# Input rows of a hybrid decoder step loaded in quarter-row transfers for pairs of token blocks

## The chip, the cores and the metric

The kernel runs on one core of a Trainium2 chip. The metric is the device time of one execution in microseconds (us); the profiler's record of one execution gives, beside it, the span from its first to its last instruction. Engines are named as in the profile: PE is TensorE (PEld its weight loads), DVE is VectorE, ACT is ScalarE, POOL is GpSimd, SP is SyncE, which here only issues transfers (DMAs).

## What is computed

One inference step of a hybrid decoder layer: a Mamba-2 branch and a gated-linear-attention branch, merged by gates, then cross-attention into 256 memory tokens, then a causal ConvFFN. The tokens are 256 of a prompt and 32 of a sample group (8 sequences of 4), 288 in all, with 2048 channels. The change lies in the first 110 us, where two things are computed side by side. One is the keys and values of the prompt's memory:

```python
def _mem_kv(mem, norm_mem, w_ck, w_cv):
    mn = _rmsnorm(mem, norm_mem)
    k = (mn @ w_ck).reshape(Bsz, N_MEM, CROSS_HEADS, CROSS_HEAD_DIM)
    v = (mn @ w_cv).reshape(Bsz, N_MEM, CROSS_HEADS, CROSS_HEAD_DIM)
```

The other is the first norm of the layer, `xn = _rmsnorm(x, p['norm_mix'])`, whose result, turned so that channels lie on partitions, is what all input projections multiply.

## The kernel before

**Weights.** All weights are float32 and stream from HBM once. `wload` (L108) brings a piece of 128 x 2 x 512 numbers (512 KB) into one of three `raw` buffers (`RB = 3`), on SP's queue. `wsplit` (L100) makes two parts of each half of a piece: ACT casts it to `whi` (L103), DVE subtracts to get `wlo` (L105). There are five buffers of each (`WB = 5`). PE then does six matmuls of 128 x 512 for each half in `mem_proj` (L321, L322, L325). A new piece may be issued when DVE has made the second `wlo` of the piece three places ahead, whose buffer it takes over. So PE, ACT, DVE and SP form a loop through three buffers.

**The stage of the change.** `mem_proj` runs first for head 0 of `w_ck` (it also loads the memory tokens into `mt`), then L467 weaves four more projections (`w_cv` head 0, `w_ck` head 1, `w_cv` head 1, `w_ck` head 2: 32 pieces in all) with a background generator, one step of it for about one half piece. The background is `x_norm` (L388) and then `x_prep` (L435).

**The input rows.** `xrow` (L362) is a tile of 128 x 9 x 512: nine blocks of 32 tokens. Token t of a block has the i-th quarter of its row (512 channels, 2 KB) on partition 32 i + t. `x_load(n)` (L382) loads one block, the sample's first (block 8), then the prompt's blocks 0 to 7, at steps 3, 6, 9, ... 27 of `x_norm`. At step 12 `square` begins: for each block ACT sums squares (L393) and DVE turns 32 x 32 squares of it into `xT` (L395), block 8 first, then 0 to 7 at steps 15 to 36. Once all are there, one matmul (L429) spreads the sums, and `x_prep` scales, splits and stores x (L439 to L443).

**What sets the order.** The steps are written out by hand in program order. SP issues in that order: each weight piece and each x transfer stands in one line, and an instruction that waits holds all those behind it. SP's transfers count their landings on eight semaphores in turn (DMAHW0 to DMAHW7), so a transfer also can't be issued before the one eight places ahead of it on the queue has landed. An x load depends on nothing but its place on the queue and on `mt`, whose memory `xrow` takes over.

Of the kernel before, what the change touches and what calls it, by code (L numbers as in the profile page):

```python
# [42 lines left out]
def hybrid_step(ctx: ExitStack, tc: tile.TileContext, I: dict, O: list):  # L43
    ctx.enter_context(tc.block(schedule_with_timeline_sim=True))
    nc = tc.nc
# [20 lines left out]
    def mm_tile():  # L66
        return ps.tile([P, 512], F32, tag="mm", bufs=3, name="mm")
# [27 lines left out]
    def vec(name):  # L95
        o, n = vofs[name]
        return vcol[:, o:o + n]
# [174 lines left out]
    with pool("p0") as p0:  # L272
# [89 lines left out]
        xrow = p0.tile([P, 9, 512], F32, tag="rows", name="xrow")  # L362
# [18 lines left out]

        def x_load(n):  # L382

            b = n - 1 if n else 8
            src = I["x_prompt"][0, 32 * b:32 * b + 32] if n else I["x_sample"].rearrange("b l d -> (b l) d")
            tc.keep_in_program_order(nc.sync.dma_start(out=xrow[:, b, :], in_=src.rearrange("t (i d) -> i t d", i=4)))

        def x_norm():  # L388
            ss = p0.tile([P, 9], F32, name="ss")

            def square(b):
                junk = p0.tile([P, 512], F32, name="junk")
                tc.keep_in_program_order(S.activation(junk, xrow[:, b, :], ACT.Square, accum_out=ss[:, b:b + 1]))  # L393
                tc.keep_in_program_order(
                    V.transpose(xT[:, :, 32 * b:32 * b + 32], xrow[:, b, :].rearrange("p (x j) -> p j x", j=KT)))  # L395

            for step in range(37):
                if step % 3 == 0 and 3 <= step <= 27:
                    x_load(step // 3 - 1)
                if step == 3:  # L400

                    V.tensor_reduce(mrs, mss, AX.X, ALU.add)
                    S.activation(mrs, mrs, ACT.Ln, scale=1.0 / D, bias=epsc[:, 0:1])
                    S.activation(mrs, mrs, ACT.Exp, scale=-0.5)
                if step == 6:
                    held.pop()()
                if step % 3 == 0 and step >= 12:
                    square(step // 3 - 5 if step > 12 else 8)
                yield
            yield  # L410
            a = mm_tile()
            TR(a[:, 0:r], vrow[0:r, :], ident[0:r, 0:r])
            TR(a[:, 128:224], crow, ident[0:96, 0:96])
            yield
            V.tensor_copy(vcol[:, 0:r], a[:, 0:r])
            V.tensor_scalar(scw, a[:, 128:224], 0.5, None, ALU.mult)
            ob, nb_ = vofs["ssd_conv_b"]
            V.tensor_scalar(vcol[:, ob:ob + nb_], vcol[:, ob:ob + nb_], 0.5, None, ALU.mult)
            V.tensor_scalar(rg, vec("gla_norm"), 0.5, None, ALU.mult)
            for e in range(2):  # L420
                V.tensor_copy(dcol[64 * e:64 * e + 64, :],
                              drow[64 * e:64 * e + 64, :].rearrange("p (t e) -> p e t", e=2)[:, e, :])
            yield

            dg = p0.tile([P, 9, NS], F32, name="dg")
            V.tensor_tensor(dg, fold4.unsqueeze(1).to_broadcast([P, 9, NS]), ss.unsqueeze(2).to_broadcast([P, 9, NS]), ALU.mult)
            yield
            a = mm_tile()
            MM(a[:, 0:T], ones, dg.rearrange("p c t -> p (c t)"), start=True, stop=True)  # L429
            S.activation(rtok, a[:, 0:T], ACT.Ln, scale=1.0 / D, bias=epsc[:, 0:1])  # L430
            S.activation(rtok, rtok, ACT.Exp, scale=-0.5)
# [22 lines left out]
        for c in range(4):  # L454
# [11 lines left out]
        V.tensor_copy(gmask, gm_f)  # L466
        weave(chain(*(mem_proj(*a) for a in ((I["w_cv"], 0, o_pmv), (I["w_ck"], 1, o_pmk), (I["w_cv"], 1, o_pmv),  # L467
                                             (I["w_ck"], 2, o_pmk)))), chain(x_norm(), x_prep()), 4 * KT - 2, 59)


# [772 lines left out]
    for n in range(8):  # L1243
        kind, i = units[n]
# [64 lines left out]
    for q in range(4):  # L1309
        m = pc.tile([P, 4, T], F32, tag="mar", bufs=2, name="mar")  # L1310
# [288 lines left out]
    for i in range(5):  # L1599
        src = I["ffn_conv_w"][i] if i < 3 else I["ffn_conv_b"] if i == 3 else I["norm_final"]  # L1600
# [223 lines left out]
```

## Time and profile before

| | before |
|---|---|
| time, median of 3 runs | 2531.62 us (2530.82 to 2531.65) |
| time of the profiled execution | 2531.55 us |
| its span | 2529.8 us |
| PE busy | 2499.2 us, 99% of the span |
| DVE, ACT, POOL busy | 1755.3, 1336.4, 393.3 us |
| moved by DMA | 521.95 MB, mean 206 GB/s |

The span is 1.75 us shorter than the execution's own time. Times in the trace count from the span's start. Rows of the windows view give, for a stretch, each engine's busy time and instructions, the granted TensorE clock (1.00 is full), the mean busy share of the 16 DMA engines, and what they moved. In the views of waits a row reads: who waited, for whom, total us, times, longest. In the timeline a bracket at the end of a row gives the idle time before it and what ended it. In the chain of waits, a DMA row lasts from the issue of a transfer to its landing.

### The profile page before, as it was taken

Reading aid. Unit: us, or ns where it says so; the run is one execution under the profiler, and the core shown is the slowest. Engines: PE = TensorE matmul, PEld = TensorE weight load, DVE = VectorE, ACT = ScalarE, POOL = GpSimd, SP = SyncE. Lnnn points to the kernel's source line nnn. Section 1 sums busy time; section 2 is a strip of 40 time slices with the busy share of each in tenths; the row PEclk is TensorE's granted clock in tenths of the full one; section 3 lists DMA queues with packets and bytes.
Section 4 is the critical chain, followed back from the end, with each engine's and each line's share of the span. In section 5 each row is a group of like instructions: output and inputs, shape, how many; then the busy total and the mean of one; then the engine's idle time right before and its main releaser. Section 6 shows DMA issues by size and latency. Waiting matters only on the chain.

```text
span 2529.8 us, 50295 instructions
## 1 busy us (share of the span) xinstructions
PE 2499.2 (99%) x18866; PEld 2405.9 (95%) x18866; DVE 1755.3 (69%) x3757; ACT 1336.4 (53%) x2714; POOL 393.3 (16%) x728
## 2 busy tenths in 40 slices
PE   8999999999999999999999999999999999999998
PEld 7789999999999999999999988999999999999998
DVE  5766677787867656666666677667777677675765
ACT  5655647655363645454454544555555455454545
POOL 3011043332300000000001112402111001020010
PEclk9999999999999999999999999999999999999999
DMA  7766687867868676767677698655555555555554
GB/s 228 255 197 194 179 250 205 232 190 231 236 188 271 184 244 182 247 204 264 205 227 244 197 329 316 210 164 174 169 173 169 170 171 173 167 171 172 169 170 129
DMA packets 442009, 521.95 MB, mean 206 GB/s; under 512 B 26768, under 2 KB 390128, under 8 KB 441732
## 3 DMA queue, kind: packets, MB, share of 16 engines
q1 hardware_dynamic: 407716, 422.34, 54.6%
q0 software_dynamic: 34016, 96.38, 11.9%
q8 instruction: 148, 2.42, 0.4%
q14 instruction: 97, 0.79, 0.1%
q10 hardware_dynamic: 32, 0.01, 0.0%
HBM read 473.13 MB, written 45.48 MB: 205 GB/s over the span
## 4 chain that ended last, share of the span: by engine, by line
PE 90%; DMA 5%; DVE 2%; ACT 1%; issue 1%; POOL 0%; SPq 0%; DVEq 0%; ACTq 0%
PE acc L148 26%; PE acc L147 26%; PE acc L151 26%; PE acc L321 2%; PE acc L325 2%; PE acc L322 2%; DMA raw<-in_w_cv_dram 1%; DMA raw<-in_w_ck_dram 1%; DVE wlo L105 1%; PE mm L1152 1%; PE la L1143 1%; PE la L1476 1%; DMA raw<-in_w_in_dram 1%; PE mm L1116 1%; DMA raw<-in_w_cq_dram 1%
## 5 line engine op out<-in xcount | busy, mean ns | idle before, releaser
L103 ACT CAST whi<-raw 128x512 fp32r<-128x512 f32 x1464 | 895.1, 618 | 1034.1 <-PE acc L148 759.0
L105 DVE TENSOR_TENSOR wlo<-raw,whi 128x512 fp32r<-128x512 f32 x1464 | 996.4, 688 | 614.2 <-ACT whi L103 599.9
L147 PE MATMUL acc<-xn,whi 128*128 128x288 f32 (+1 forms) x1936 | 550.6, 300 | 0.0
L148 PE MATMUL acc<-xn,whi 128*128 128x288 f32 (+1 forms) x1936 | 542.6, 296 | 0.0
L151 PE MATMUL acc<-xn,wlo 128*128 128x288 f32 (+1 forms) x1936 | 414.1, 295 | 0.0
L148 PE MATMUL acc<-hf,whi 128*128 128x288 f32 x1408 | 393.5, 296 | 0.0
L147 PE MATMUL acc<-hf,whi 128*128 128x288 f32 x1408 | 389.1, 292 | 0.0
L147 PEld LDWEIGHTS acc<-xn,whi 128*128 128x128 f32 (+1 forms) x1936 | 364.7, 188 | 9.9 <-issue 8.3
L148 PEld LDWEIGHTS acc<-xn,whi 128*128 128x128 f32 (+1 forms) x1936 | 365.1, 189 | 6.6 <-issue 4.6
L151 PEld LDWEIGHTS acc<-xn,wlo 128*128 128x128 f32 (+1 forms) x1936 | 311.1, 188 | 1.7 <-issue 1.3
L151 PE MATMUL acc<-hf,wlo 128*128 128x288 f32 x1408 | 295.0, 290 | 0.0
L148 PEld LDWEIGHTS acc<-hf,whi 128*128 128x128 f32 x1408 | 265.0, 188 | 0.1
L147 PEld LDWEIGHTS acc<-hf,whi 128*128 128x128 f32 x1408 | 264.3, 188 | 0.1
L151 PEld LDWEIGHTS acc<-hf,wlo 128*128 128x128 f32 x1408 | 226.6, 188 | 0.0
L148 PE MATMUL acc<-pr,whi 128*128 128x288 f32 x704 | 196.7, 296 | 0.0
L147 PE MATMUL acc<-pr,whi 128*128 128x288 f32 x704 | 195.0, 293 | 0.0
L151 PE MATMUL acc<-pr,wlo 128*128 128x288 f32 x704 | 147.7, 290 | 0.0
L147 PE MATMUL acc<-un,whi 128*128 128x288 f32 x512 | 145.5, 300 | 1.4 <-DVE mb L954 1.2
L148 PE MATMUL acc<-un,whi 128*128 128x288 f32 x512 | 143.1, 295 | 0.0
L1648 POOL COPY fsp<-fst 128x16 f32<-128x16 f32 x88 | 37.1, 425 | 656.1 <-DVE av L1660 402.1
L148 PEld LDWEIGHTS acc<-pr,whi 128*128 128x128 f32 x704 | 132.5, 188 | 0.0
L147 PEld LDWEIGHTS acc<-pr,whi 128*128 128x128 f32 x704 | 132.1, 188 | 0.0
(507 smaller groups left out, 4265.3 us busy)
## 6 DMA issues: line engine op xcount, KB each, us to landing
raw<-in_w_in_dram SPq DMA_DIRECT2D x240, 512.0 KB
raw<-in_w_up_dram SPq DMA_DIRECT2D x176, 512.0 KB
raw<-in_w_down_dram SPq DMA_DIRECT2D x88, 512.0 KB
raw<-in_w_cv_dram SPq DMA_DIRECT2D x32, 512.0 KB
raw<-in_w_ssd_out_dram SPq DMA_DIRECT2D x32, 512.0 KB
sin<-in_state_gla_dram POOLq DMA_DIRECT2D x32, 512.0 KB, 6.0
out_dram<-sin SPq DMA_DIRECT2D x32, 512.0 KB
raw<-in_w_gla_out_dram SPq DMA_DIRECT2D x32, 512.0 KB
```

The source lines that it names most:

```text
L103: S.copy(hi, raw)
L105: V.tensor_tensor(lo, raw, hi, ALU.subtract)
L147: MM(a, hi[:, k, cs], xh, start=(k0 + s0 + k == 0), stop=False)
L148: MM(a, hi[:, k, cs], xl, start=False, stop=False)
L151: MM(a, lo[:, k, cs], xh, start=False, stop=(k0 + s0 + k == nk - 1))
L321: MM(accs[m], mn_hi[:, kk, ms_], hi[:, 0, :], start=(kk == 0), stop=False)
L322: MM(accs[m], mn_lo[:, kk, ms_], hi[:, 0, :], start=False, stop=False)
L325: MM(accs[m], mn_hi[:, kk, ms_], lo[:, 0, :], start=False, stop=(kk == KT - 1))
L1116: MM(a, kt[:, i, k * P:(k + 1) * P], vt[i], start=True, stop=True)
L1143: MM(osa[NS * j:NS * j + NS, :], qdm[:, k, b, :], sins[b][:, k, :], start=False, stop=(q == 1 and k == 0))
L1152: MM(a, kb[:, k * P:(k + 1) * P], vst, start=True, stop=True)
L1648: G.tensor_copy(sp[:, :, 0:2], st.rearrange("p (b k) -> p b k", k=2))
```

## The change

`x_load` now loads two blocks of the prompt at once (the sample's block alone), and does so with four transfers, one for each quarter of the row: 32 partitions, on each 2 x 2 KB. Before, it was one transfer for a block, with the quarters as the outermost dimension (4), then 32 tokens, then 512 channels. Now the outermost dimension of each transfer is 32. The loads stand at steps 3 (sample), 6, 12, 18 and 24. Bytes and places in SBUF are the same; 9 transfers become 20.

```diff
         def x_load(n):
-            b = n - 1 if n else 8
-            src = I["x_prompt"][0, 32 * b:32 * b + 32] if n else I["x_sample"].rearrange("b l d -> (b l) d")
-            tc.keep_in_program_order(nc.sync.dma_start(out=xrow[:, b, :], in_=src.rearrange("t (i d) -> i t d", i=4)))
+            b, m = (2 * n - 2, 2) if n else (8, 1)
+            src = I["x_prompt"][0, 32 * b:32 * b + 64] if n else I["x_sample"].rearrange("b l d -> (b l) d")
+            for i in range(4):
+                tc.keep_in_program_order(nc.sync.dma_start(
+                    out=xrow[32 * i:32 * i + 32, b:b + m, :],
+                    in_=src[:, 512 * i:512 * i + 512].rearrange("(b t) d -> t b d", t=32)))
...
             for step in range(37):
-                if step % 3 == 0 and 3 <= step <= 27:
-                    x_load(step // 3 - 1)
+                if step == 3 or step % 6 == 0 and 6 <= step <= 24:
+                    x_load(step // 6)
```

On PE, DVE, ACT and POOL every instruction stands where it stood; only lines behind L386 move by three. On SP, this is the queue at the start of the woven stage, before (`raw` is a weight piece, `xrow` an x load; x3 means three such in a row):

```order
17 L114 DMA raw<-in_w_cv_dram 128x2x512 x3
18 L386 DMA xrow<-in_x_sample_dram 128x1x512
19 L114 DMA raw<-in_w_cv_dram 128x2x512
20 L386 DMA xrow<-in_x_prompt_dram 128x1x512
21 L114 DMA raw<-in_w_cv_dram 128x2x512 x2
22 L386 DMA xrow<-in_x_prompt_dram 128x1x512
23 L114 DMA raw<-in_w_cv_dram 128x2x512
24 L386 DMA xrow<-in_x_prompt_dram 128x1x512
25 L114 DMA raw<-in_w_cv_dram 128x2x512
26 L114 DMA raw<-in_w_ck_dram 128x2x512
27 L386 DMA xrow<-in_x_prompt_dram 128x1x512
28 L114 DMA raw<-in_w_ck_dram 128x2x512
```

And the same place on SP with the change:

```order
17 L114 DMA raw<-in_w_cv_dram 128x2x512 x3
18 L387 DMA xrow<-in_x_sample_dram 32x512 x4
19 L114 DMA raw<-in_w_cv_dram 128x2x512
20 L387 DMA xrow<-in_x_prompt_dram 32x2x512 x4
21 L114 DMA raw<-in_w_cv_dram 128x2x512 x3
22 L387 DMA xrow<-in_x_prompt_dram 32x2x512 x4
23 L114 DMA raw<-in_w_cv_dram 128x2x512
24 L114 DMA raw<-in_w_ck_dram 128x2x512 x2
25 L387 DMA xrow<-in_x_prompt_dram 32x2x512 x4
26 L114 DMA raw<-in_w_ck_dram 128x2x512 x4
27 L387 DMA xrow<-in_x_prompt_dram 32x2x512 x4
```

The weight pieces stand in the same order; a group of four x transfers comes after every third or fourth of them, where one came after every one or two.

With the semaphores that each waits for, the same queue from the sample's load on, before (DVE is the wait for the `raw` buffer, a DMAHW number the wait for a landing):

```order
20 L386 DMA xrow<-in_x_sample_dram 128x1x512 [waits DMAHW6_49,DMAHW0_49,PE_49]
21 L114 DMA raw<-in_w_cv_dram 128x2x512 [waits DMAHW2_49,DVE_49]
22 L386 DMA xrow<-in_x_prompt_dram 128x1x512
23 L114 DMA raw<-in_w_cv_dram 128x2x512 [waits DMAHW3_49,DVE_49]
24 L114 DMA raw<-in_w_cv_dram 128x2x512 [waits DMAHW4_49,DVE_49]
```

And with the change, where the piece just ahead of the sample's load counts on DMAHW4 and the sample's four on DMAHW5, 6, 7 and 0:

```order
20 L387 DMA xrow<-in_x_sample_dram 32x512 [waits DMAHW6_49,DMAHW0_49,PE_49]
21 L387 DMA xrow<-in_x_sample_dram 32x512 x3
22 L114 DMA raw<-in_w_cv_dram 128x2x512 [waits DMAHW2_49,DVE_49]
23 L387 DMA xrow<-in_x_prompt_dram 32x2x512
24 L387 DMA xrow<-in_x_prompt_dram 32x2x512 [waits DMAHW3_49]
25 L387 DMA xrow<-in_x_prompt_dram 32x2x512 [waits DMAHW4_49]
26 L387 DMA xrow<-in_x_prompt_dram 32x2x512 [waits DMAHW5_49]
27 L114 DMA raw<-in_w_cv_dram 128x2x512 [waits DMAHW6_49,DVE_49]
28 L114 DMA raw<-in_w_cv_dram 128x2x512 [waits DMAHW7_49,DVE_49]
```

The third and fourth transfer of the first pair now wait for the landing of that piece and of the sample's first transfer, and the next weight piece stands behind them.

## The prediction

> **What bounds the kernel now.** I read the page first, then the waits of PE, then the windows of the stage where those waits lie, then the chain of waits, then DMA shares in windows of a few us.
>
> ```profile
> PE 2499.2 (99%) x18866; PEld 2405.9 (95%) x18866; DVE 1755.3 (69%) x3757; ACT 1336.4 (53%) x2714; POOL 393.3 (16%) x728
> ...
> PE acc L321 <- ACT whi L103: 9.7, 7, 1.6
> ...
> core 0: us, PE busy (x) PEld busy (x) DVE busy (x) ACT busy (x) POOL busy (x), PEclk, DMA share, GB/s
> 41.00:90.00 49.00, 39.33 (x165) 29.91 (x164) 24.81 (x36) 22.23 (x46) 0.73 (x1) 1.00 0.66 211
> 90.00:140.00 50.00, 50.00 (x244) 42.28 (x243) 39.00 (x77) 32.71 (x67) 7.74 (x19) 1.00 0.79 248
> 140.00:240.00 100.00, 100.00 (x550) 87.53 (x549) 58.57 (x108) 56.57 (x107) 9.99 (x24) 1.00 0.69 208
> ```
>
> PE bounds the kernel. Of its 30.6 us without work (2529.8 less 2499.2), 9.7 are in seven waits for `whi`, all between 41 and 90 us, which is when the x loads run; from 90 to 240 us PE is never idle. So this stage is where an x load can cost or bring time. What does `whi` wait for? The waits of ACT from 41 to 90 us and one stall in the timeline answer it:
>
> ```profile
> ACT whi L103 <- DMA raw<-in_w_ck_dram: 12.9, 5, 3.9
> ACT whi L103 <- DMA raw<-in_w_cv_dram: 11.1, 4, 4.3
> ...
> 34.18 0.38 SPq L114 DMA_DIRECT2D raw<-in_w_cv_dram  x1
> 34.61 0.58 SPq L386 DMA_DIRECT2D xrow<-in_x_prompt_dram  x1
> 35.29 0.43 SPq L114 DMA_DIRECT2D raw<-in_w_cv_dram  x1
> ...
> 42.94 1.14 ACT L103 CAST whi<-raw 128x512 fp32r<-128x512 f32 x2 [4.31 <-DMA raw<-in_w_cv_dram]
> 43.61 0.51 PE L321 MATMUL acc<-whi,mn_hi 128*128 128x512 f32 x1 [1.59 <-ACT whi L103]
> ```
>
> For landings of weights. The piece issued at 34.18 us, behind the sample's x load, is cast only at 42.94, and PE starts 1.59 us late. How long pieces fly, and what the loop through the three buffers adds, is in the chain of waits (a DMA row lasts from issue to landing):
>
> ```profile
> 32.87 4.54 DMA raw<-in_w_cv_dram
> ...
> 39.46 9.14 DMA raw<-in_w_cv_dram
> ...
> 49.42 7.93 DMA raw<-in_w_cv_dram
> ...
> 64.50 7.65 DMA raw<-in_w_ck_dram
> ...
> 72.26 0.63 ACT whi L103
> ...
> 73.52 0.70 DVE wlo L105
> 74.23 11.44 DMA raw<-in_w_ck_dram
> ...
> 88.10 0.23 PE acc L321
> ...
> 89.46 0.23 PE acc L321
> ```
>
> PE needs 89.46 - 88.10 = 1.36 us for six matmuls, a half piece, so 2.73 us for a piece and 8.18 us for the three in the buffers. From a landing (64.50 + 7.65 = 72.15) to the next issue into that buffer (74.23) go 2.08 us. So PE is fed as long as a piece flies no longer than 8.18 - 2.08 = **6.1 us**. The four long flights have a mean of 9.04: the loop then gives a piece every (9.04 + 2.08)/3 = 3.71 us. Measured: 165 matmuls are 13.75 pieces in 49 us, 3.56 us each. The loop explains the stage within 4%.
>
> Why 8 to 11 us, when 4.54 occurs? DMA shares in stretches inside the stage, against one with x stores and weights but no x load:
>
> ```profile
> 44.50:45.00 0.50, 0.50 (x4) 0.41 (x3) 0.39 (x1) 0.00 (x0) 0.00 (x0) 1.00 0.26 94
> 58.00:60.00 2.00, 1.88 (x8) 1.58 (x9) 1.90 (x4) 1.90 (x6) 0.00 (x0) 1.00 0.26 102
> 68.00:70.50 2.50, 2.49 (x10) 1.70 (x10) 1.52 (x3) 2.50 (x6) 0.73 (x1) 1.00 0.26 102
> 79.00:81.00 2.00, 1.94 (x9) 1.20 (x7) 1.16 (x2) 0.00 (x1) 0.00 (x0) 1.00 0.26 101
> 100.00:120.00 20.00, 20.00 (x91) 16.48 (x90) 15.45 (x31) 13.57 (x28) 0.71 (x1) 1.00 0.97 336
> ```
>
> A share of 0.26 is 4.2 of 16 engines, at 102 GB/s: for 2 us at a time four engines work and twelve are empty. Four is the outermost dimension of the x transfer. So 256 KB take 2.6 us on four engines, and a weight piece, which has a part on all 16, lands only when its parts behind that x load are through, with the next x load queued behind it again. From 100 to 120 us, x stores of 288 KB (128 partitions) lie between the same weight pieces at 336 GB/s, and PE is busy for all 20 us.
>
> **The change, part by part.** *Removed: the queue on four engines.* With 32 outermost, I take each quarter transfer to spread over 16 engines. No row of before shows an x transfer of this shape, so its speed is bounded: below by the four-engine rows (102 GB/s), above by the full-width y stores at the end; the nearest row is that of the last y store, of 32 partitions, alone in the second window:
>
> ```profile
> 2522.83 2.39 SPq L1780 DMA_DIRECT2D out_dram<-y  x2
> ...
> 2525.00:2526.50 1.50, 0.00 (x0) 0.00 (x0) 0.00 (x0) 0.00 (x0) 0.00 (x0) 0.50 1.00 401
> 2527.50:2528.00 0.50, 0.00 (x0) 0.00 (x0) 0.00 (x0) 0.00 (x0) 0.00 (x0) 0.50 1.24 295
> ```
>
> I take 295 GB/s: a pair of blocks (512 KB) is 1.8 us of all engines, once in three or four pieces. A piece right behind it flies at most 4.54 + 1.8 = 6.3 us, the others 4.54; the mean, about 5, is under the bound of 6.1, and the five `whi`/`wlo` buffers (five half pieces, 6.8 us of PE) absorb one late piece. So PE should be fed throughout.
>
> The Trainium skill, page "DMA: Bandwidth & Descriptors", section "Why a DMA increments its semaphore by 16 and not by 1", says that a transfer runs on the largest number of engines up to 16 that divides the outermost sizes of both sides. By it the transfers go from 4 engines to 16; the row of 0.26 agrees for the 4, and no run here shows the 16 yet.
>
> What is that worth? At PE's pace, 165 matmuls take 165 x 1.364/6 = 37.4 us of the 49, so **11.6 us** are lost. This is more than the 9.7 us of waits, since in each of seven stalls PE also drains (0.39 less 0.23 us) and restarts slowly (0.51 less 0.39): 7 x 0.28 = 2.0, sum 11.7.
>
> *Added: issues on SP.*
>
> ```profile
> L386 SPq DMA_DIRECT2D xrow<-in_x_prompt_dram x8: 558/569/1012, 34.6 to 72.2; - x8
> L386 SPq DMA_DIRECT2D xrow<-in_x_sample_dram x1: 737/737/737, 33.3 to 33.3; - x1
> ...
> L114 SPq DMA_DIRECT2D raw<-in_w_cv_dram x32: 367/368/427, 25.5 to 194.5; - x32
> ...
> L507 SPq DMA_DIRECT2D acum_d<-acumT x1: 344/344/344, 148.8 to 148.8; - x1
> ...
> L601 SPq DMA_DIRECT2D out_dram<-cst x16: 737/792/848, 238.7 to 577.9; - x16
> ```
>
> A quarter transfer lies between 0.34 (L507, 32 partitions) and 0.79 us (L601, 3 or 24 partitions). I take 0.4, near L507 and the weight pieces: 20 x 0.4 = 8.0 against 0.74 + 8 x 0.57 = 5.3 us, 2.7 more on SP in 49 us, of which its weight issues take 14 x 0.37. SP has room. A weight piece behind a group comes 4 x 0.4 = 1.6 us later instead of 0.57, which lies inside the cushion of the buffers. At 0.79 the group holds it 3.2 us, still less.
>
> *Added: waits on SP.* The third and fourth transfer of the first pair wait for the piece of 32.87 (landed 32.87 + 4.54 = 37.41) and for the sample's first quarter. Behind them on SP stand the weight pieces. The next, issued at 35.29 before, then goes at 37.41 + 2 x 0.4 = 38.2 and lands at 42.8. PE wants it 2.73 us after 41.86 (where it now stalls: 43.61 less 1.59, less 0.16 of drain), so its cast must start by 44.6 - 0.67 = 43.9. 1.1 us are to spare; with 6.1 us of flight it would be 0.4 late. In later groups the transfer eight places ahead lies three weight pieces back, 3 x 2.73 = 8.2 us, and has landed. For this and single late pieces I leave **0.6 us** (bounds 0 and 5.8, half of the loss).
>
> *Moved: arrival of x.* Odd blocks come three steps earlier, none later. The first use is far behind:
>
> ```profile
> 53.66 0.63 ACT L393 ACTIVATE junk<-xrow 128x512 f32<-128x512 f32 x1
> ```
>
> The sample's load was issued 20 us ahead. Nothing is won or lost here.
>
> **Sum**, against the profiled execution (2531.55 us: span 2529.8 and 1.75 around it; the median, 2531.62, is 0.07 above): 2531.55 - 11.6 + 0.6 = **2520.6 us**. PE then goes on 11 us earlier, and between 90 and 240 us nothing makes it wait that isn't itself driven by this chain.
>
> **Rivals.** (1) *Only half is won*: weights still fly 7.5 us, because quarter transfers move slower than I take. The loop gives (7.5 + 2.08)/3 = 3.19 us a piece, 13.75 x (3.19 - 2.73) = 6.3 us remain, and the time is 2531.55 - 5.3 = **2526.2**. For it: the share of 1.24 at 295 GB/s, packets slower than those of full-width stores. Against it: x is a quarter of the stage's bytes (9 x 256 KB beside 14 x 512 KB). The Trainium skill, "SBUF — State Buffer", section "Door 1: The DMA port swizzle", says that 32 partitions reach 8 of the 16 ports, so such a transfer runs at half rate, about 218 GB/s. By that, my estimate is 2.4 us for a pair where the row of 295 GB/s gives 1.8; the row of the last y store agrees that it is slower, but by a quarter, not a half.
>
> (2) *The gain is given back*: PE, 11 us earlier, meets something with a time of its own, and ends near **2531.5**. Against it: no wait of PE from 90 to 240 us, and buffers set when later loads start.
>
> (3) *Slower*: the transfers do not do what the change says and still go over four engines. Then flights stay near 9 us, nothing is won, and the new wait bites: the third transfer stands on SP until 32.87 + 9.0 = 41.9, the next piece is issued at 42.7 and lands at 51.7, where PE wants it at 43.9: some 7.8 us, against about 1 us of stall that this piece has now, so **2538.4**. It decides once flights stay above 6.1 us on the mean. Against it: the share follows the outermost dimension, and 0.26 fits 4.
>
> **Chances.** Forecast 0.72 (2519 to 2523), (1) 0.13 (2523 to 2527), (2) 0.07 (2527 to 2532), (3) 0.08 (2532 to 2540). A measurement of this kernel tells some 0.2%, 5.1 us, from no change: faster means below 2526.5. The forecast and nearly all of (1) lie there: faster 0.84, same 0.09, slower 0.07. The range is 2518.8 (all of 11.6 and 1 us more, from matmul records that may be missing in 165) to 2526.5, which leaves out (2), (3) and the edge of (1).
>
> **What will show it.** Right: no stretch at a share of 0.26 and 102 GB/s in the stage; PE's waits for `whi` there fall from 9.7 us to under 2; ACT's waits for `raw` shrink; four x issues in a row of about 0.4 us; the spread matmul (L429 before) starts some 11 us earlier. Wrong: shares of 0.26 still there (rival 3), or shares over 1 while PE still waits (rival 1), or PE's waits gone here and as much idle time behind 90 us (rival 2).

## The result, and the profile after

The changed kernel takes 2519.92 us (median of 4 runs, 2516.15 to 2523.97), against 2531.22 (4 runs, 2529.74 to 2531.65) before: a ratio of 0.9957, with a 95% interval of 0.9939 to 0.9974. Two later sets of runs, each beside new runs of before, gave 0.9971 (0.9957 to 0.9985) and 0.9967 (0.9956 to 0.9979). So it is faster by 0.3 to 0.4%, 7 to 11 us. The forecast was 2520.6. The 65 runs of before in the later sets have medians of 2527.14 to 2529.04 us, and all lie between 2520.79 and 2536.57 but for one slow run of 2718.35 us; so the four runs of before in the first set lie high, and the first difference, 11.3 us, is the largest of the three (the others are 7.7 and 6.9).

The profiled execution of the changed kernel is the longest of its four, 2523.97 us, span 2522.2. Read again the waits of PE over the whole span (us, number of waits, the longest):

```profile
PE mm L890 <- ACT cst L599: 2.4, 1, 2.4
PE acc L321 <- ACT whi L103: 2.2, 3, 1.6
```

and the window of the stage, with the busy time of each engine, the granted clock, the DMA share and GB/s:

```profile
41.00:90.00 49.00, 46.64 (x200) 36.65 (x199) 31.36 (x46) 27.99 (x58) 1.45 (x2) 1.00 0.84 248
```

The waits for `whi` fell from 9.7 us in seven to 2.2 in three, and are no longer the longest of the kernel. In the same 49 us PE does 200 matmuls instead of 165; at 0.227 us each 3.5 us are still lost where 11.6 were. DMA moves 248 GB/s in the stage instead of 211, and no stretch at a share of 0.26 and 102 GB/s is left between 33 and 99 us. The spread matmul that ends the stage (`dg`, 128x288) comes 8.2 us earlier; the first row is of before, the second of after:

```profile
L429 PE MATMUL mm<-dg,ones x2: 403/405/407, 107.0 to 107.2; 128*128 128x288 f32 x2
```

```profile
L432 PE MATMUL mm<-dg,ones x2: 403/405/407, 98.8 to 99.1; 128*128 128x288 f32 x2
```

Where SP issues x, and what flights of weights the chain of waits still shows between 30 and 90 us of the changed kernel:

```profile
32.71 0.37 SPq L114 DMA_DIRECT2D raw<-in_w_cv_dram  x1
33.18 1.80 SPq L387 DMA_DIRECT2D xrow<-in_x_sample_dram  x4
35.08 0.38 SPq L114 DMA_DIRECT2D raw<-in_w_cv_dram  x1
35.51 2.16 SPq L387 DMA_DIRECT2D xrow<-in_x_prompt_dram  x4
37.76 0.89 SPq L114 DMA_DIRECT2D raw<-in_w_cv_dram  x1
```

```profile
32.71 4.14 DMA raw<-in_w_cv_dram
...
37.76 8.00 DMA raw<-in_w_cv_dram
...
68.63 6.16 DMA raw<-in_w_ck_dram
```

Three weight landings are left in the chain where five were, and the one of 8.00 us is the piece behind the sample and the first pair, which have one weight piece between them. It makes the longest stall left:

```profile
45.86 1.14 ACT L103 CAST whi<-raw 128x512 fp32r<-128x512 f32 x2 [3.42 <-DMA raw<-in_w_cv_dram]
46.53 0.50 PE L321 MATMUL acc<-whi,mn_hi 128*128 128x512 f32 x1 [1.55 <-ACT whi L103]
```

Since 33.18 us SP had issued 768 KB of x and a weight piece of 512 KB ahead of it, of which a part had still to move, and POOL was storing 512 KB at the same time (`out_dram<-mp`, issued at 36.03 us, in before at 36.20). How fast quarter transfers move is seen better in two later stretches, in which a pair and some weights move. They are from the changed kernel; the row behind them is from experiment e3 below, whose x transfers write to all 128 partitions (by the order on the queue and the 512 KB moved, it holds two of these transfers):

```profile
47.00:49.00 2.00, 2.00 (x11) 1.59 (x10) 1.35 (x3) 1.14 (x2) 0.00 (x0) 1.00 0.99 203
55.50:60.50 5.00, 5.00 (x23) 4.14 (x23) 2.39 (x4) 1.87 (x5) 0.00 (x0) 1.00 1.08 203
```

```profile
53.60:55.20 1.60, 1.60 (x9) 1.33 (x8) 1.60 (x3) 1.05 (x4) 0.00 (x0) 1.00 1.00 324
```

The share is about 1 in all three, but with quarter transfers 203 GB/s move, with full-width ones 324. The Trainium skill, page "SBUF — State Buffer", section "Door 1: The DMA port swizzle", has about 218 GB/s for 32 partitions, which reach 8 of 16 ports. The 203 GB/s agree with that figure; the full-width transfers here do not reach twice as much. That x is read in pieces of 2 KB does not by itself explain the low rate: before read the same pieces at 102 GB/s on four of 16 engines, a quarter of the 401 GB/s that the full-width y stores reach at a share of 1.00.

### The profile page after: what moved, and what is told of

It is laid out like the page before. It is cut to its first block, busy times and chain, and to the rows that moved or that the text cites. A ratio compares the mean times of both kernels' runs of the same rounds, so it can differ in the third digit from the quotient of the medians.

```text
span 2522.2 us, 50312 instructions
## 1 busy us (share of the span) xinstructions
PE 2500.9 (99%) x18866; PEld 2409.0 (96%) x18866; DVE 1756.2 (70%) x3757; ACT 1335.8 (53%) x2714; POOL 393.6 (16%) x728
## 4 chain that ended last, share of the span: by engine, by line
PE 96%; DMA 1%; DVE 1%; ACT 1%; issue 0%; POOL 0%; SPq 0%; DVEq 0%; ACTq 0%
PE acc L148 28%; PE acc L147 27%; PE acc L151 27%; PE acc L321 2%; PE acc L325 2%; PE acc L322 2%; PE la L1537 1%; PE mm L1155 1%; PE la L1146 1%; PE mm L1119 1%; PE la L1479 1%; DMA raw<-in_w_cv_dram 0%; PE la L864 0%; PE mm L1130 0%; PE mm L1127 0%
```

## The experiments

Theory WIDTH: weights were late because an x transfer with 4 outermost sits on four engines, and the parts of weight pieces behind it wait there. Rival PLACE: fewer and earlier interruptions by x are what helped. Theory PORTS, for what is left: transfers to 32 partitions run at half rate. Waits are PE's for `whi` in the stage (us, times); "spread" is the start of the `dg` matmul, which depends only on what PE did up to there, and not on its pace later on. Each is from the one profiled execution of that run.

| run | median us | ratio to before (95%) | waits | spread, us |
|---|---|---|---|---|
| before | 2531.22 | | 9.7, 7 | 107.0 |
| after | 2519.92 | 0.9957 (0.9939 to 0.9974) | 2.2, 3 | 98.8 |
| e1, four engines at after's places | 2533.99 | 1.0034 (1.0023 to 1.0045) | 12.4, 6 | 114.3 |
| e2, quarters at before's places | 2519.82 | 0.9977 (0.9963 to 0.9992) | 1.9, 2 | 97.2 |
| e3, full width | 2515.47 | 0.9955 (0.9943 to 0.9966) | 0.4, 1 | 95.7 |
| e4, after again | 2519.41 | 0.9971 (0.9957 to 0.9985) | 1.7, 3 | 96.9 |
| e5, pairs three steps later | 2515.29 | 0.9962 (0.9949 to 0.9975) | 0.3, 1 | 95.3 |
| e6, order 0, 2, 1, 3 | 2516.89 | 0.9952 (0.9934 to 0.9970) | 2.0, 2 | 98.1 |
| e7, half on ACT's queue | 2521.22 | 0.9975 (0.9965 to 0.9984) | 2.4, 3 | 98.6 |
| e8, before, each block twice | 2548.69 | 1.0088 (1.0071 to 1.0104) | 22.3, 9 | 129.8 |
| e9, before's transfers from POOL | 2525.88 | 0.9990 (0.9979 to 1.0001) | 5.2, 4 | 102.3 |
| e10, e5 again | 2515.84 | 0.9950 (0.9937 to 0.9964) | none | 94.2 |
| e11, after again | 2522.10 | 0.9967 (0.9956 to 0.9979) | 1.9, 3 | 97.3 |

The ratios of e1 to e4, e5 to e8 and e9 to e11 go by the runs of before beside them (medians 2527.14, 2527.42 and 2529.04).

**e1 and e2: the two halves of the change apart.** e1 keeps the places and takes back the shape:

```diff
-            for i in range(4):
-                tc.keep_in_program_order(nc.sync.dma_start(
-                    out=xrow[32 * i:32 * i + 32, b:b + m, :],
-                    in_=src[:, 512 * i:512 * i + 512].rearrange("(b t) d -> t b d", t=32)))
+            for a in range(m):
+                tc.keep_in_program_order(nc.sync.dma_start(
+                    out=xrow[:, b + a, :], in_=src[32 * a:32 * a + 32].rearrange("t (i d) -> i t d", i=4)))
```

> Each block is loaded by one transfer as before (4 outermost, on four engines), but the loads stand at the changed kernel's places: two blocks in a row at steps 6, 12, 18 and 24. Theory WIDTH (weights are late because their parts queue behind x on four engines): no gain, 2531 us within 3, stretches of 0.26 DMA share still there, PE's waits for whi near 9.7 us or more, since two blocks in a row hold four engines for 5 us. Theory PLACE (fewer, earlier interruptions of the weights are what helps): 2520 to 2524 us, waits for whi at 2 to 4 us.

Measured: slower than before, 12.4 us of waits, up to 4.6 us in one. The four-engine stretches are there again, and behind pauses of PE its granted clock is at half for some us (two windows of e1):

```profile
62.50:63.50 1.00, 0.88 (x4) 0.73 (x5) 0.90 (x2) 0.90 (x3) 0.00 (x0) 1.00 0.26 102
...
45.60:49.00 3.40, 3.40 (x9) 2.13 (x7) 0.13 (x1) 0.00 (x0) 0.00 (x0) 0.50 0.63 198
```

e2 keeps before's places and takes the shape, 36 transfers:

```diff
-            tc.keep_in_program_order(nc.sync.dma_start(out=xrow[:, b, :], in_=src.rearrange("t (i d) -> i t d", i=4)))
+            for i in range(4):
+                tc.keep_in_program_order(nc.sync.dma_start(
+                    out=xrow[32 * i:32 * i + 32, b, :], in_=src[:, 512 * i:512 * i + 512]))
```

> Four quarter transfers of 32 partitions, but for each single block and at the places of before (steps 3 to 27): 36 transfers instead of 9. WIDTH: as the changed kernel, 2518 to 2522 us, no stretch of 0.26 share. PLACE: no gain, 2529 to 2533 us. If the number of issues on SP is what costs (36 x 0.41 = 15 us of SP), slower than the changed kernel by some us and weight issues late.

Measured: as the changed kernel, in waits, in the stage and in time. With before, after and e1 these are all four combinations of shape and places: at either place the new shape is faster by some 7 us or more, and the places alone cost (e1 against before, 1.0034). So the shape makes the gain. PLACE falls, and so does the number of issues as a cost: 36 at a median of 0.43 us did no harm.

**e3: the outermost dimension alone, and the ports.** Against e1 only the outermost dimension differs, and with it the partition on which each quarter row lands:

```diff
             for a in range(m):
                 tc.keep_in_program_order(nc.sync.dma_start(
-                    out=xrow[:, b + a, :], in_=src[32 * a:32 * a + 32].rearrange("t (i d) -> i t d", i=4)))
+                    out=xrow[:, b + a, :], in_=src[32 * a:32 * a + 32].rearrange("t (i d) -> (t i) d", i=4)))
```

> One transfer per block at the changed kernel's places, with 128 outermost on both sides, so that each quarter row stands on partition 4 t + i instead of 32 i + t: x's rows stand in the wrong places, so everything computed from them is changed, the work is the same. Against e1 only the outermost dimension differs. WIDTH: as the changed kernel or better, 2516 to 2521 us. Theory PORTS (in the changed kernel 2 KB packets to 32 partitions took 158 to 196 ns instead of 84, some 200 GB/s, and the 2.2 us of waits for whi left there come from it): packets near 84 ns, DMA share about 1 at 350 to 400 GB/s during x, waits for whi under 1 us, 2 to 3 us below the changed kernel. PLACE: as the changed kernel.

Measured: the same 9 transfers at the same places in one transfer for a block, and the spread matmul starts at 95.7 us instead of 114.3. This is WIDTH with no transfer moved. Waits fall to 0.4 us, below the 2.2 and 1.7 of quarter transfers, as PORTS had it. The two x transfers in the row of e3 above move at 324 GB/s, less than the 350 to 400 expected; between 40 and 44 us DMA reaches 408 GB/s, but there nearly all of it is weights and POOL's store. With fewer issues the piece behind the first pair also goes out earlier in e3 (35.53 us instead of 37.76), so e3 does not separate the rate from the issues and waits on SP. The kernel can't use this layout, since its results are not those of the step.

**e4 and e11: the changed kernel again.** No edit.

> The changed kernel once more, to see what varies: four executions so far spread from 2516.2 to 2524.0 us where before spread by 1.9 us. If the stalls in the stage vary: waits for whi between 0 and 4 us and the rest equal. If it is the pace of matmuls elsewhere (in the profiled execution 134 instead of 131.7 ns a matmul from 1250 to 1450 us, worth some 5 us): the time varies while the start of the spread matmul L432 stays near 98.8 us.

> The changed kernel, for the comparison with e10: waits for whi at 1.7 to 2.2 us, L432 at 97 to 99 us, time 2514 to 2527 us with a median near 2519.

Measured: the stage varies little (spread at 98.8, 96.9 and 97.3 us), the total much (2514.07 to 2526.82). Most of it arises in one stretch, the merge and the cross-attention projections. There PE does the same instructions at another pace without being idle. The rows are of before, after, e4 and e5:

```profile
1260.00:1360.00 100.00, 100.00 (x761) 100.00 (x760) 66.87 (x124) 50.73 (x97) 9.27 (x15) 1.00 0.75 236
```

```profile
1260.00:1360.00 100.00, 100.00 (x746) 100.00 (x745) 64.50 (x118) 48.55 (x92) 9.61 (x16) 1.00 0.73 239
```

```profile
1260.00:1360.00 100.00, 100.00 (x746) 100.00 (x746) 64.70 (x118) 48.57 (x91) 9.94 (x15) 1.00 0.76 239
```

```profile
1260.00:1360.00 100.00, 100.00 (x771) 100.00 (x771) 65.73 (x122) 48.99 (x94) 9.78 (x15) 1.00 0.77 244
```

761, 746 and 771 matmuls in 100 us at a granted clock of 1.00: a matmul takes 131.4, 134.0 or 129.7 ns. The work from the last `mb` of the merge to the first `qs` of cross-attention, the same in every run, took 217.7 us in before, 222.2 in after, 222.3 in e4 and 215.0 in e5: up to 7.3 us of total that have nothing to do with x. The executions of e4, e6, e3 and after, all at 746, took 2523.97 to 2529.55 us, those of e2 and e5 at 772 and 771 took 2516.98 and 2515.72. This is not the only such place: PE's wait for `cst` between 560 and 590 us is 1.6 us in e10 and e11, 2.4 in after and 4.9 in e6.

**e5 and e10: the loads spread out.**

```diff
-                if step == 3 or step % 6 == 0 and 6 <= step <= 24:
-                    x_load(step // 6)
+                if step == 3 or step % 6 == 3 and 9 <= step <= 27:
+                    x_load((step - 3) // 6)
```

> The changed kernel with the four pair loads three steps later (9, 15, 21, 27 instead of 6, 12, 18, 24), so that the sample's and the first pair's transfers no longer stand behind one another. Theory BUNCH (the 1.6 us stall left at 46.5 us comes from 768 KB of x between the same two weight pieces): that stall goes, waits for whi at 0 to 1 us, spread matmul L432 at 95 to 97 us, 1 to 2 us less than the changed kernel. Theory PORTS alone (what is left comes from the half rate of 32-partition transfers wherever they stand): waits for whi stay at 1.7 to 2.2 us, L432 at 97 to 99 us.

> The version of e5 (pair loads three steps later) once more, beside the changed kernel in the same call: waits for whi at 0 to 1 us, L432 near 95.3 us; in the total 1 to 3 us below the changed kernel, if the pace of matmuls from 1150 to 1430 us (130.0, 131.7 or 134.4 ns in the executions so far, worth up to 9 us) does not cover it.

Measured: 0.3 us of waits in e5, none in e10. In e5, x still moves at a low rate (two stretches below), yet PE is busy throughout; in e10 it does 218 matmuls in the stage's 49 us, which is its full pace (49/0.227 = 216).

```profile
44.00:48.00 4.00, 4.00 (x19) 3.33 (x18) 1.87 (x4) 1.14 (x2) 0.00 (x0) 1.00 1.02 231
51.00:55.00 4.00, 4.00 (x19) 3.29 (x19) 3.31 (x6) 2.64 (x8) 0.00 (x0) 1.00 1.06 227
```

```profile
41.00:90.00 49.00, 49.00 (x218) 40.55 (x217) 33.07 (x48) 28.84 (x60) 1.45 (x2) 1.00 0.91 281
```

So the low rate alone costs next to nothing here; most of what the changed kernel still loses comes from the first pair standing close behind the sample's group, not between the same weight pieces, as the expectation says, but with a single one between. Without the pair ahead of it, that weight piece goes out at 35.40 us in e5 instead of 37.76; what the bytes ahead of it and what the four issues and their wait on SP had cost was not separated. This version beats both kernels in the stage (spread at 95.3 and 94.2 us). In the total, beside the same runs of before, its ratio of 0.9950 lies under e11's 0.9967, with intervals that still overlap, and the medians are 6.3 us apart.

**e6 and e7: both halves of the partitions at a time.** e6 only changes the order:

```diff
-            for i in range(4):
+            for i in (0, 2, 1, 3):
```

> The changed kernel with the quarters issued in the order 0, 2, 1, 3, so that neighbours on the queue write to partitions 64 apart. By PORTS, if engines run ahead of one another enough to overlap neighbours: 2 KB packets fall from 158 to 196 ns to nearer 100 ns and waits for whi to under 1 us. If all 16 engines keep in step within one transfer: no difference, packets at 150 to 200 ns, waits for whi at 1.7 to 2.2 us.

Measured: no difference in the stage (waits 2.0, spread 98.1), and the stretches are as slow. Its median lies lower than after's, but its five runs go from 2514.08 to 2529.55, and nothing in the stage supports a gain.

```profile
47.00:49.00 2.00, 2.00 (x10) 1.66 (x9) 1.47 (x3) 0.66 (x2) 0.00 (x0) 1.00 0.93 204
55.00:59.00 4.00, 4.00 (x19) 3.31 (x18) 2.08 (x4) 1.58 (x4) 0.00 (x0) 1.00 1.03 216
```

e7 issues two of the four from ACT:

```diff
-                tc.keep_in_program_order(nc.sync.dma_start(
+                tc.keep_in_program_order((nc.sync if i < 2 else S).dma_start(
```

> The changed kernel with quarters 2 and 3 issued from ACT's queue at the same steps, two by SP and two by ACT, so that both halves of the partitions are written at a time. PORTS: packets near 100 ns while both run, waits for whi under 1 us as far as the weights go. Against it: ACT issues 10 transfers at some 0.4 us between its casts and waits for landings there, so casts may come late; up to 3 us of new waits of PE for whi that no landing of a weight explains. Time 2516 to 2523 us.

Measured: 283 GB/s from 47 to 49 us instead of 203, which may be overlap (or more weights in the same 2 us), but 2.4 us of waits, among them two, ending at 42.5 and 56.3 us, where the changed kernel has none. What the faster transfers bring, ACT's issues and waits may take; the two were not separated.

```profile
47.00:49.00 2.00, 2.00 (x11) 1.59 (x9) 0.59 (x1) 0.19 (x1) 0.00 (x0) 1.00 1.03 283
```

**e8: the suspected cost doubled.**

```diff
             tc.keep_in_program_order(nc.sync.dma_start(out=xrow[:, b, :], in_=src.rearrange("t (i d) -> i t d", i=4)))
+            tc.keep_in_program_order(nc.sync.dma_start(out=xtwo[:, n % 2, :], in_=src.rearrange("t (i d) -> i t d", i=4)))
```

> The kernel before with each block's transfer issued twice, the second into a spare tile that nobody reads. WIDTH: each extra transfer holds four engines for 2.6 us, 9 x 2.6 = 23.6 us more in the queue that the weights stand in; the stage is queue-bound, so PE's waits for whi grow from 9.7 to 25 to 33 us and the time to 2545 to 2555 us. If the four engines were not the bound of the stage, less than 5 us more.

Measured: 2548.69 us, 21 more than the runs of before beside it (2527.42), and the spread matmul 22.8 us later, near the forecast of nine transfers at 2.6 us (23.6). The waits (22.3 us) are less than the 25 expected: they grew by 12.6 of the 22.8 us. The rest fits the time at half clock, since the mean granted clock is 0.83 from 41 to 120 us, where before had 1.00:

```profile
41.00:120.00 79.00, 56.70 (x194) 42.64 (x193) 32.16 (x46) 28.58 (x58) 1.45 (x2) 0.83 0.57 191
```

**e9: x off SP's queue.**

```diff
-            tc.keep_in_program_order(nc.sync.dma_start(out=xrow[:, b, :], in_=src.rearrange("t (i d) -> i t d", i=4)))
+            tc.keep_in_program_order(G.dma_start(out=xrow[:, b, :], in_=src.rearrange("t (i d) -> i t d", i=4)))
```

> The transfers of before (one for each block, 4 outermost), issued from POOL, whose queue is otherwise nearly idle here, so that x no longer stands ahead of weights on SP's queue; they all go early. If what made weights late is standing behind x in one queue, and engines serve two queues in turn: four engines at 102 GB/s give weights some 51 GB/s, a piece's quarter (128 KB) each 2.6 us, just PE's pace of 2.73: waits for whi 0 to 3 us, time near the changed kernel, 2515 to 2522 us. If a queue of x on four engines delays weights from any queue: waits 8 to 15 us, 2527 to 2535 us. If the share of 0.26 doesn't show, POOL's transfers go over more engines and the test tells the width again.

Measured: 5.2 us of waits, between the two expectations, and a share near 1 while x moves:

```profile
33.00:50.00 17.00, 13.75 (x53) 10.55 (x52) 4.94 (x9) 5.72 (x13) 2.15 (x3) 0.90 0.97 241
```

POOL issues x early (the sample at 31.3 us), and an x transfer then takes 12.1 us at the median to land, so several are under way at once. The share suggests that together they hold more than four engines; no row shows which. In the total, 0.9990 with an interval up to 1.0001, e9 can't be told from before. This does not tell order in one queue from the load on the engines; that stays open.

## Why the prediction was right, step by step

- **The bound of the stage**: that x on four engines makes the weights late is shown. e1 against e3 changes the outermost dimension alone and moves the stage by 18.6 us; e8 adds nine more such transfers and 22.8 us. The bound of 6.1 us of flight, from three buffers, was not tested by itself. The three flights left agree with it roughly: 4.14 us without a stall, 6.16 with 0.48 us, 8.00 with 1.55.
- **16 engines for 32 outermost**, which no row of before showed: the stretches of 0.26 are gone, and the share is 0.99 and 1.08 in the two stretches with x shown above.
- **The rate of quarter transfers was mis-sized**: 295 GB/s taken, 203 measured with some weights in it, so a pair takes about 2.6 us, not 1.8. The row behind the 295 is 0.5 us of a store, at a share of 1.24. The same store of before over 0.75 us has 229 GB/s, which the prediction does not show and which is near what was measured:

```profile
2527.25:2528.00 0.75, 0.00 (x0) 0.00 (x0) 0.00 (x0) 0.00 (x0) 0.00 (x0) 0.50 0.94 229
```

  The estimate of 2.4 us for a pair in rival 1 was the nearer one.
- **SP's issues**: 0.4 us taken; 425 ns at the median for the pairs. SP is no bound, as said.
- **The wait of the third and fourth transfer**: the piece behind them went out at 37.76 us (38.2 forecast). It was to land at 42.8 with 1.1 us to spare. It flew 8.00 us instead of 4.54, and PE stalled 1.55 us. The order was right, the flight was not: quarter transfers move at about two thirds of the rate taken (203 of 295 GB/s), and POOL's store of 512 KB, which the prediction left out, moved at the same time. What each added to the 8.00 us was not measured. This stall is most of why 3.5 us were lost in the profiled stage instead of the 0.6 I left; e5, with no pair ahead of that piece, loses almost nothing.
- **The sum**: the stage gave 8.2 us in the profiled run and 10.1 and 9.7 in e4 and e11, not 11.0. In e4 PE waits another 0.87 us for `whi` at 136 us, where the prediction saw nothing to wait for. That the median fell within 0.7 us of the forecast is luck in part. The sum starts from the profiled execution of before, 2531.55 us, and that of the changed kernel took 2523.97, 7.6 us less, in the band of rival 1. In the later sets, where before is faster, the whole gain is 7.7 and 6.9 us. All these totals hold the pace of matmuls later on, which the prediction did not know.
- **What PE does with the gain**: the last `mb` of the merge is at 1204.3 us instead of 1214.6, so 10.3 us are carried there. Between the two, before had a half clock that after did not have:

```profile
560.00:590.00 30.00, 27.52 (x197) 26.67 (x197) 24.68 (x61) 10.04 (x21) 16.18 (x26) 0.94 1.04 293
```

```profile
560.00:590.00 30.00, 27.62 (x209) 26.78 (x208) 23.14 (x55) 11.44 (x23) 10.17 (x15) 1.00 0.98 296
```

  (before, then after: 0.06 of 30 us is 1.8 us.) From there to the first `qs` of cross-attention (1426.5 instead of 1432.3 us) 4.5 us went in the slower matmuls. Nothing of size waits in place of the stalls that went: PE's time without work fell from 30.6 to 21.3 us over the whole span. So rival 2 fell.
- **Rival 1** had the right mechanism (slow quarter transfers) and not the size: it left 6.3 us of loss in the stage, the forecast 0.6, and 3.5 were measured. **Rival 3** is what e1 built, nearly: at 1.0034 of before it ended on the slower side.

## What to carry to other kernels

Look at the mean DMA share next to the rate: here a share stuck at a quarter with a quarter of the rate came from transfers whose outermost dimension is 4, and the wide transfers behind them on that queue came late. Give such a transfer an outermost dimension that spreads it (four times the issues did no harm here), and space groups of them so that a buffered stream does not have two of them close ahead of one piece. And where totals vary by several us, judge a stage by its own end, not by the total.

## What the runs showed of the hardware that was not expected

- The same matmul stream ran at 129.7, 131.4 or 134.0 ns a matmul from 1260 to 1360 us, in different executions of the same program too (after: 746 matmuls in 100 us; the same kernel in e11: 762), at a granted clock of 1.00 and with PE never idle. What chooses the pace stays open.
- Around and behind pauses of PE of 2 to 5 us lie 3.4 us or more at a granted clock of 0.50: in e1 from 45.6 to 49.0 us, shortly behind a wait of 2.33 us that ended at 44.45, and again from 89.9, behind one of 4.6 us; in e8 from 44.0 to 50.8, with a wait of 4.23 us that ended at 45.78. The waits near 577 us differ: around those of 2.5 us in before and 2.2 us in e4 the mean clock from 560 to 590 us is 0.94, around that of 2.4 us in after it is 1.00.
- In stretches with transfers of 32 partitions, 203 GB/s moved at a share of 1.08, where two transfers of 128 partitions moved at 324 with a share of 1.00.
